# Short-sequence scores of two query tiles in one row-half visit, in an order that plans TensorE's operands as late

## The chip, the cores and the metric

One core of one Trainium2 chip runs the whole program in one launch. The metric is the device time of one execution in microseconds, as the median of several runs.

## What is computed

One layer of a hybrid encoder for two sequences, 256 and 512 rows of width 1024 in fp32, worked on together as 768 columns. Cut to what matters:

```
xn   = rmsnorm(x);  proj = xn @ w_in
y_a  = RWKV-7 mixer, 16 heads, one scan forward and one backward
y_b  = differential attention, 8 heads, partial rotary
h    = x + (sigmoid(ga) * (y_a @ proj_a) + sigmoid(gb) * (y_b @ proj_b)) @ w_out
y    = rmsnorm(h + relu(rmsnorm(h) @ w_mlp_in)**2 @ w_mlp_out)

def attend(qblk):                       # for each head, for each 128 queries
    s = einsum('bhcqd,bhckd->bhcqk', qblk, k)      # c = 0, 1; d = 64
    p = softmax(s, axis=-1)
    att = p[:, :, 0] - lam * p[:, :, 1]
    return einsum('bhqk,bhkv->bhqv', att, v)
```

## The kernel before, in words

The program is written once as a list of operations, each with the engines that could run it. A planner, `Plan.schedule`, then walks that list in Python with modelled durations and decides, for every engine, the order in which its operations are issued. On the chip every engine runs its list in that order and waits by semaphores. So no time of the model is on the chip; what the model leaves there is the order alone, and an operation that stands early in its engine's list holds up all that stand behind it until its operands are there.

What the planner goes by, as far as this case needs it:

- When an operation ends, each of its users becomes ready at that end plus `AFTER` of the user's engine (line 131); for TensorE that is 0.053 us.
- Among the operations that are ready, an engine takes the one with the smallest key: the stage's base number plus `SHIFT` of its label (line 577). On TensorE `SWITCH` (1.24, line 135) is added if the operation uses another tile shape of the array than the last one (128x128, the row halves 64x128, 128x64, 32x32).
- `BIAS` weighs the engines that could run an operation, and `LATE` (line 575) says how many pieces of the late work (the last 16 projections, then the product with proj_a) are put ahead of each attention head.

The stages in order of time:

1. The input is normalised and transposed (0 to 30 us), and the first projections run.
2. The RWKV stage, up to about 1085 us of the profile. Eight pairs of heads, four jobs each (two directions, two halves), 32 jobs in all. A job makes its operands (`front`), multiplies them on TensorE (`g1`), solves triangular systems (`solve`), and then runs through its six chunks (`duo`, `chain`). The solve goes from the products through a DMA to GpSimd, where it is 62 small tensor operations of 96 partitions (line 622, tiles named f), and by a DMA back into tiles that VectorE transposes (line 677). Its result is first read by TensorE in products of 128x64 array tiles, then 32x32. A chunk of `chain` is a pair of 128x64 products whose result is copied and read by the next pair. `fill` (line 658) zeroes the first state of a sequence on GpSimd. Projections of 128x384 columns (tile x) fill TensorE in between; `proj_shift` also adds shifted columns on GpSimd (128x256), and `front` adds one 128x384 tile there for every second job.
3. The attention stage (to about 1290 us), with the late work between. For each head and each 128 queries: scores of both halves c, their maxima on VectorE, exponentials on ScalarE, the difference, transposes, and the product with v. The two score products contract over 64 rows each and lie in different row halves of the array, where they run side by side; each fills a PSUM bank of its own. This is done twice per head for the short sequence (256 columns) and four times for the long one (512).
4. proj_b, w_out and the second norm (to about 1480 us), then the MLP.

A transpose on TensorE is line 698, every other matmul line 693. An fp32 product shows as two matmul rows, one of the projections (fp32r) as one.

Of the kernel before, what the change touches and what calls it, by code (L numbers as in the profile page):

```python
# [19 lines left out]
P = 128  # L20
D = 1024
TP, TS = 256, 512
# [4 lines left out]
C = 64  # L27
# [100 lines left out]
    return out  # L128


AFTER = dict(pe=0.053, act=0.034, dve=0.033, pool=0.077, sp=0.026)
TAIL = dict(dve=0.09, act=0.1, pool=0.03)
HELD = 0.012
PORT = 0.16
SWITCH = 1.24


DEBUG = {}
# [168 lines left out]
class Plan:  # L307
# [99 lines left out]
    def schedule(self):  # L407
# [14 lines left out]
        def blocked(o):  # L422
            for b in o.take:
                p = b.pool
                if p.lock or (p.ordered and p.next != b.n):
                    return p
                if b.pin is None and len(p.free) < sum(c.pool is p for c in o.take) or b.pin is not None and all(i != b.pin for _, i in p.free):
                    return p
            return None

# [35 lines left out]
        def choose(e, t):  # L466

            switch = lambda o: SWITCH * (e == "pe" and o.forms[e][2][0] != clock.tile)
            for k, n, r, o in sorted((o.key + TURN * turns(o, e) + switch(o), o.n, r, o) for r, o in avail[e] if r <= t + 1e-3):
# [12 lines left out]
        while len(order) < len(self.ops):  # L482
# [8 lines left out]
            if best is None:  # L491
                t, e = ways[0]
                best = min((x for x in avail[e] if x[0] <= t + 1e-3), key=lambda x: (x[1].key, x[1].n))
            r, o = best
            withdraw(o)
            p = blocked(o)
# [3 lines left out]
            for b in o.take:  # L500
                p = b.pool
# [39 lines left out]
            for s in o.next:  # L541
                s.wait -= 1
                for f in s.forms:
                    s.ready[f] = max(s.ready[f], clk[e] if e == f == "pe" else end + AFTER[f])
                if not s.wait:
# [3 lines left out]
            for b in o.blocks:  # L549
# [4 lines left out]
                if not b.left:  # L554
                    p = b.pool
# [16 lines left out]
WSTEP = 2  # L572
LATEKEY = 1.0
NLATE = 16
LATE = (4, 4, 4, 3, 3, 4, 4, 2)
REGIONS = dict(h=352, x=18816, f=12304, g1=6400, g2=15336)
SHIFT = {'proja': 3.64, 'rotate': -7.5, 'vs': -19.94, 'attn': -2.04, 'solve': -1.61, 'attend': -3.24, 'kkn': -4.92, 'proj': 4.76, 'g1': 1.9, 'g2': -1.95, 'chain': 1.9, 'norm': -6.88, 'x': -4.47, 'const': -7.99, 'lora': -10.39, 'front': 0.93, 'duo': -2.19, 'finish': -0.48, 'extra': 0.92, 'head': 3.89, 'projb': -6.52, 'wout': 18.65, 'mlp': -1.8}
BIAS = {'x': {'dve': -0.25, 'act': 0.68, 'pool': -0.82}, 'a': {'dve': 2.31, 'pool': 5.49, 'act': -0.17}, 'b': {'dve': 0.49, 'pool': 4.32, 'act': -0.19}, 'c': {'act': -0.05, 'pool': 1.31, 'dve': 0.09}}
RINGS = dict(fq=1, wraw=3, w=3, tst=3, X=2, g2r=2, vs=2, ik=3, sa=2, mk=1, y3=1, fo=2, v=2, k=2, r=2, lora=1, lr=1, py=1, cr=1)


def layer(tc, I, O, mark=None):
# [6 lines left out]
    size = lambda a: int(np.prod(a.shape[1:]))  # L589
# [93 lines left out]
    def mm(out, lhsT, rhs, start=True, stop=True, after=()):  # L683

        n, m, k = size(rhs), size(lhsT), lhsT.shape[0]
        if rhs.dtype == F32R:
            us, tail = max(0.118, n / 2400 + 0.0135), 0.25
        else:
            us, tail = 2 * max(n / 1200 + 0.005, 0.112 if m > 64 else 0.058), 0.165
        tile = tuple(next(x for x in (32, 64, 128) if y <= x) for y in (k, m))  # L690
        row, col = lhsT.quarter()[1], out.quarter()[1]
        slot = {(C, P): row // 2, (P, C): col // 2, (C, C): row // 2 * 2 + col // 2, (32, 32): row}.get(tile, 0)
        emit = lambda: TE.matmul(chip(out), lhsT=chip(lhsT), rhs=chip(rhs), start=start, stop=stop)  # L693
        pl.op([("pe", us, emit, (tile, rhs.dtype != F32R, slot))], [lhsT, rhs], [out], tail=tail, after=after)
        return pl.ops[-1]
# [12 lines left out]
    new = pl.block  # L708
# [6 lines left out]
    def bank(shape, co=()):  # L715
        return new(PS, shape, co=co)

    halves = [slice(h * HALF, (h + 1) * HALF) for h in range(2)]
    H0, H1 = slice(0, C), slice(C, P)
# [12 lines left out]
    o = 0  # L732
    for n, src, a, b in (
# [8 lines left out]
        so, w = PAR[src]  # L742
# [209 lines left out]
    extra = [QK0 + 4 * g for g in range(4)]  # L952
# [333 lines left out]
    pe_ = [pool_b([P, TS], 3) for i in range(2)]  # L1286
    pmx = pool_b([P, 4], 4)
# [3 lines left out]
    def load_head(h):  # L1291
# [17 lines left out]
            cpy(v[:, u : u + 3], ps)  # L1309
        return res + [v]  # L1310

    def attend(h, q, k, v):
        at("attend", h, key=200.0 + h)
        oT = yb[h]
        for t0, n in ((0, TP), (TP, TS)):
            nk = n // P
            for qt in range(nk):
                qo = slice(qt % 2 * P, qt % 2 * P + P)
                if qt % 2 == 0:
                    ah = new(pah, [P, 4, TP])  # L1320
                qs = slice(t0 + qt * P, t0 + (qt + 1) * P)
                ks = slice(t0, t0 + n)
                ms = new(pmx, [P, 4])
                mx, sm = ms[:, 0:2], ms[:, 2:4]
                e = [new(pe_[c], [P, TS])[:, 0:n] for c in range(2)]
                sc = [bank([P, n], [e[1], ms])]
                sc.insert(0, bank([P, n], [e[0], ms, sc[0]]))
                for c in range(2):
                    R = slice(c * C, (c + 1) * C)
                    mm(sc[c], q[R, qs], k[R, ks])  # L1330
                for c in range(2):
                    reduce(mx[:, c : c + 1], sc[c], ALU.max)
                ts(mx, mx, -0.125, None, ALU.mult, ALU.bypass)
                for c in range(2):
                    act(e[c], sc[c], AF.Exp, scale=0.125, bias=mx[:, c : c + 1], accum_out=sm[:, c : c + 1])
                recip(sm)
                tt(sm[:, 1:2], sm[:, 1:2], nlam, ALU.mult)
                scale(e[1], sm[:, 1:2])
                stt(e[0], e[0], sm[:, 0:1], e[1], ALU.mult, ALU.add)
                ps = bank([P, nk, P], [ah])  # L1340
                for u in range(nk):
                    tr(ps[:, u], e[0][:, u * P : (u + 1) * P])
                cpy(ah[:, 0:nk, qo], ps)
                if qt % 2 == 0:
                    continue
                ps = bank([P, TP], [oT])
                for u in range(nk):
                    kt = t0 // P + u
                    mm(ps, v[:, kt], ah[:, u], u == 0, u == nk - 1)
                q0 = t0 + (qt - 1) * P  # L1350
                cpy(oT[:, q0 : q0 + TP], ps)
        sq = new(psq, [P, T])
        tt(sq, oT, oT, ALU.mult, *AB)
        for b in range(2):
            ps = bank([P, HALF])
            mm(ps, ones, sq[:, halves[b]])
            act(sq[:, halves[b]], ps, AF.Ln, scale=1.0 / P, bias=eps[:, 2:3])
        act(sq, sq, AF.Exp, scale=-0.5)
        tt(oT, oT, sq, ALU.mult, *AB)
# [61 lines left out]
    for now in range(8):  # L1421
        for _ in zip(range(LATE[now]), more):
            pass
# [23 lines left out]
    for h in range(8):  # L1447
# [4 lines left out]
        for b in range(2):  # L1452
            c = halves[b]
# [41 lines left out]
    pss = [bank([P, 512]) for t in range(6)]  # L1495
    tok = [slice(t * P, (t + 1) * P) for t in range(6)]
    for k in range(KD):
        w = load_rows(I["wo"][0, :, k, :])
# [4 lines left out]
    pss = [bank([P, 512]) for t in range(6)]  # L1503
# [19 lines left out]
    for fb in range(NFB):  # L1523
        at("mlp", fb, key=600.0 + fb)
        hid = new(pmg, [P, 4, 2, T])
        for f in range(4):
            ps = gemm(load_w(I["w1"][4 * fb + f]), hn, [hid])
            for b in range(2):
                c = halves[b]
# [4 lines left out]
        for half in range(2):  # L1534
            c = slice(half * 512, (half + 1) * 512)
# [68 lines left out]
```

## Time and profile before

| | before |
|---|---|
| median of 3 runs | 1998.9 us |
| lowest and highest | 1997.29 and 1999.33 us |
| the profiled execution's own time | 1998.35 us |
| its span, first to last instruction | 1996.5 us |
| TensorE busy | 1938.1 us (97%) |
| VectorE, ScalarE, GpSimd busy | 1259.4, 871.9, 828.5 us |
| mean granted clock of TensorE | 0.989 |

Busy time on TensorE is taken from modelled ends that reach past the next start, so 97% is not an array at its peak. Lines are those of the kernel above. PE is TensorE's matmuls, PEld its weight loads, DVE is VectorE, ACT ScalarE, POOL GpSimd, SP the queue of most DMAs.

### The profile page before, as it was taken

How to read it: one execution, taken by the hardware profiler on the slowest of the kernel's cores; microseconds unless marked ns; L12 is line 12 of the kernel's file. 1: busy time of each engine (PE TensorE's matmuls, PEld its weight loads, DVE VectorE, ACT ScalarE, POOL GpSimd, SP SyncE). 2: the span in 40 equal slices, each digit the busy share in tenths (PEclk: the TensorE clock that was granted, in tenths of full speed). 3: DMA queues.
4: the chain of work that ended last, by engine and by line, in shares of the span. 5: the costliest groups of instructions: out<-in, count | busy, mean ns of one | idle time of the engine just before them, and what ended most of it. 6: DMA issues, size and time to landing. Idle time of an engine off the chain costs nothing.

```text
span 1996.5 us, 36368 instructions
## 1 busy us (share of the span) xinstructions
PE 1938.1 (97%) x12698; PEld 1729.2 (87%) x12698; DVE 1259.4 (63%) x2750; ACT 871.9 (44%) x2178; POOL 828.5 (41%) x2177
## 2 busy tenths in 40 slices
PE   6999989999999999999999999999999999999998
PEld 6988879888888989889888776899899899989997
DVE  6977575666767677577534878574475555555545
ACT  5635465555656556565444778442221111111113
POOL 3278778786877878888770011011100000000000
PEclk9999999999999999999999999999999999999999
DMA  4133332222323232232343342254121111111111
GB/s 152 55 110 97 86 84 75 76 70 73 92 66 98 76 79 80 81 88 59 93 121 107 107 143 76 81 174 139 45 85 64 63 64 64 64 64 64 64 48 64
DMA packets 209787, 169.09 MB, mean 85 GB/s; under 512 B 106817, under 2 KB 176194, under 8 KB 209602
## 3 DMA queue, kind: packets, MB, share of 16 engines
q1 hardware_dynamic: 209602, 166.76, 28.1%
q8 instruction: 100, 1.64, 0.4%
q14 instruction: 85, 0.70, 0.1%
HBM read 137.97 MB, written 28.70 MB: 83 GB/s over the span
## 4 chain that ended last, share of the span: by engine, by line
PE 80%; DVE 11%; DMA 3%; ACT 2%; SPq 2%; issue 2%; POOL 0%; DVEq 0%; ACTq 0%; POOLq 0%
PE bank L693 78%; DVE g L622 3%; PE bank L698 2%; DVE x L622 2%; SPq L618 2%; DVE f L627 1%; DVE f L632 1%; DMA g<-dram 1%; DVE f L622 1%; DMA g<-in_w_in_dram 1%; DVE g L632 0%; DVE f L1012 0%; ACT f L669 0%; ACT x L638 0%; DVE g L677 0%
## 5 line engine op out<-in xcount | busy, mean ns | idle before, releaser
L693 PE MATMUL bank<-x 128*128 128x384 f32 (+1 forms) x5296 | 1146.9, 362 | 13.0 <-DVE x L622 4.6
L693 PEld LDWEIGHTS bank<-x 128*128 128x128 f32 x5296 | 929.6, 189 | 113.3 <-issue 18.9
L622 POOL TENSOR_TENSOR f<-f 96x60 f32<-96x60 f32 (+25 forms) x2081 | 758.9, 367 | 241.1 <-ACT f L638 41.5
L622 DVE TENSOR_TENSOR x<-g,x 128x256 fp32r<-128x256 f32 (+3 forms) x490 | 252.6, 522 | 159.7 <-ACT x L638 149.8
L693 PE MATMUL bank<-f,g 128*128 128x384 f32 x1920 | 338.2, 337 | 1.6 <-ACT f L669 1.6
L693 PEld LDWEIGHTS bank<-f,g 128*128 128x128 f32 x1920 | 336.1, 187 | 2.6 <-ACT f L669 1.9
L638 ACT ACTIVATE x<-g 128x256 fp32r<-128x256 f32 (+2 forms) x336 | 149.8, 453 | 351.6 <-PE bank L693 282.0
L622 DVE TENSOR_TENSOR g<-bank,g 128x128 f32<-128x128 f32 (+4 forms) x380 | 178.0, 479 | 179.2 <-PE bank L693 143.2
L638 ACT ACTIVATE g<-bank 64x128 f32<-64x128 f32 (+6 forms) x659 | 203.8, 324 | 189.3 <-PE bank L693 152.8
L622 POOL TENSOR_TENSOR g<-g 128x512 f32<-128x512 f32 (+1 forms) x9 | 15.4, 1711 | 592.3 <-DVE g L622 580.8
L693 PE MATMUL bank<-g,f 128*128 128x64 f32 (+3 forms) x1568 | 245.1, 293 | 4.5 <-DVE g L622 2.1
L693 PEld LDWEIGHTS bank<-g,f 128*128 128x128 f32 x1568 | 218.1, 191 | 27.0 <-DVE f L622 3.8
L622 DVE TENSOR_TENSOR g<-g 128x384 f32<-128x384 f32 (+6 forms) x234 | 116.7, 502 | 86.2 <-ACT g L669 73.8
L669 ACT ACTIVATE g<-bank 128x384 f32<-128x384 f32 x96 | 46.3, 491 | 246.5 <-PE bank L693 246.1
L638 ACT ACTIVATE f<-bank 128x192 f32<-128x192 f32 (+6 forms) x268 | 95.4, 387 | 109.9 <-PE bank L693 95.8
L693 PEld LDWEIGHTS bank<-g,g 64*128 64x128 f32 (+1 forms) x1728 | 119.7, 193 | 22.5 <-ACT g L638 10.7
L693 PE MATMUL bank<-g,g 64*128 64x128 f32 (+1 forms) x1728 | 136.5, 287 | 1.4 <-ACT g L638 1.4
L639 DVE CAST x<-g 128x384 fp32r<-128x384 f32 (+2 forms) x156 | 56.6, 364 | 54.7 <-PE bank L693 40.4
L698 PE MATMUL bank<-h,g 128*128 128x128 f32 x392 | 67.9, 294 | 19.0 <-DVE g L647 14.3
L693 PE MATMUL bank<-f 128*128 128x256 f32 (+2 forms) x352 | 86.0, 483 | 0.0
L693 PEld LDWEIGHTS bank<-g 32*32 32x32 f32 (+2 forms) x1378 | 54.8, 130 | 34.8 <-DVE g L677 14.4
L693 PE MATMUL bank<-g 32*32 32x32 f32 (+3 forms) x1378 | 73.9, 225 | 10.5 <-DVE g L677 9.0
(80 smaller groups left out, 1356.8 us busy)
## 6 DMA issues: line engine op xcount, KB each, us to landing
g<-in_w_in_dram SPq DMA_DIRECT2D x268, 128.0 KB
g<-in_w_dram SPq DMA_DIRECT2D x128, 256.0 KB
f<-dram SPq DMA_DIRECT2D x112, 192.0 KB
dram<-g SPq DMA_DIRECT2D x80, 192.0 KB
g<-in_x_dram SPq DMA_DIRECT2D x12, 512.0 KB
g<-dram SPq DMA_DIRECT2D x32, 192.0 KB
f<-dram SPq DMA_DIRECT2D x32, 144.0 KB
g<-in_pb_dram SPq DMA_DIRECT2D x16, 256.0 KB
```

Of the source, the lines that this page charges most:

```text
L618: pl.op([("sp", us, lambda: nc.sync.dma_start(out=chip(out), in_=chip(in_)), None)], [in_], [out], n / 250e3, tail)
L622: form = lambda x: (NAME[x], cost(x, (a, b), out), lambda: x.tensor_tensor(out=chip(out), in0=chip(a), in1=chip(b), op=op), None)
L627: emit = lambda: V.tensor_scalar(out=chip(out), in0=chip(a), scalar1=chip(s1), scalar2=chip(s2), op0=o0, op1=o1)
L632: emit = lambda: V.scalar_tensor_tensor(out=chip(out), in0=chip(a), scalar=chip(s), in1=chip(b), op0=o0, op1=o1)
L638: S: ("act", cost(S, (a,), out), lambda: S.activation(out=chip(out), in_=chip(a), func=AF.Copy, scale=1.0), None),
L639: V: ("dve", cost(V, (a,), out), lambda: V.tensor_copy(out=chip(out), in_=chip(a)), None),
L669: S.activation(out=chip(out), in_=chip(a), func=fn, scale=chip(scale), **k)
L693: emit = lambda: TE.matmul(chip(out), lhsT=chip(lhsT), rhs=chip(rhs), start=start, stop=stop)
L698: pl.op([("pe", 0.112, lambda: TE.transpose(chip(out), chip(a), chip(ident)), ((P, P), True, 0))], [a, ident], [out], tail=0.165)
```

## The change

The scores move into a function of their own. For the short sequence it is called once for two query tiles: each of the two banks then holds both tiles' scores of one half c, and the four products are issued in turn between the row halves, in one visit to that array shape. For the long sequence it works on one tile as before. `blocked` lets an operation take several buffers of one ordered pool at once, since the visit takes two tiles' buffers. In the planner TensorE's operands count as ready 0.4 us later than before, and a change of array shape costs a key 2.44 instead of 1.24. `LATE` has 5 instead of 3 at the fifth head. The `SHIFT` and `BIAS` tables have new values.

```diff
-AFTER = dict(pe=0.053, act=0.034, dve=0.033, pool=0.077, sp=0.026)
+AFTER = dict(pe=0.453, act=0.034, dve=0.033, pool=0.077, sp=0.026)
...
-SWITCH = 1.24
+SWITCH = 2.44
...
-                if p.lock or (p.ordered and p.next != b.n):
+                n = sum(c.pool is p for c in o.take)
+                if p.lock or (p.ordered and not p.next <= b.n < p.next + n):
                     return p
...
-LATE = (4, 4, 4, 3, 3, 4, 4, 2)
+LATE = (4, 4, 4, 3, 5, 4, 4, 2)
...
+    def scores(qs, k, co):
+
+        n = size(k)
+        w = TS // n
+        pss = []
+        for _ in range(0, len(qs), w):
+            for c in range(2):
+                pss.append(bank([P, min(w, len(qs)), n], co + pss))
+        pss.reverse()
+        last, out = (), []
+        for i, q in enumerate(qs):
+            out.append([pss[i // w * 2 + c][:, i % w] for c in range(2)])
+            for c, R in ((0, H0), (1, H1)):
+                last = [mm(out[-1][c], q[R], k[R], after=last)]
+        return out
...
+            GQ = 2 if n == TP else 1
...
-                ms = new(pmx, [P, 4])
+                if qt % GQ == 0:
+                    mss = [new(pmx, [P, 4]) for _ in range(GQ)]
+                    es = [[new(pe_[c], [P, TS])[:, 0:n] for c in range(2)] for _ in range(GQ)]
+                    scs = scores([q[:, t0 + (qt + i) * P : t0 + (qt + i + 1) * P] for i in range(GQ)], k[:, t0 : t0 + n], [x for e in es for x in e] + mss)
+                ms, e, sc = mss[qt % GQ], es[qt % GQ], scs[qt % GQ]
                 mx, sm = ms[:, 0:2], ms[:, 2:4]
-                e = [new(pe_[c], [P, TS])[:, 0:n] for c in range(2)]
-                sc = [bank([P, n], [e[1], ms])]
-                sc.insert(0, bank([P, n], [e[0], ms, sc[0]]))
-                for c in range(2):
-                    R = slice(c * C, (c + 1) * C)
-                    mm(sc[c], q[R, qs], k[R, ks])
```

The order is where most of the change lies. The first place is TensorE in the eighteenth job, three steps of its `chain`: a step is the 128x64 pair, and the 128x384 rows between are projections. Before:

```order
L693 MATMUL bank_75<-g_91,f_97 128x64 x2
L693 MATMUL bank_80<-x_88 128x384
L693 MATMUL bank_77<-x_88 128x384 x3
L693 MATMUL bank_80<-x_88 128x384
L693 MATMUL bank_75<-g_91,f_97 128x64 x2
L693 MATMUL bank_80<-x_88 128x384 x2
L693 MATMUL bank_77<-x_88 128x384
L693 MATMUL bank_75<-g_91,f_97 128x64 x2
```

With the change:

```order
L694 MATMUL bank_80<-g_91,f_97 128x64
L694 MATMUL bank_77<-x_88 128x384 x3
L694 MATMUL bank_82<-x_88 128x384 x3
L694 MATMUL bank_80<-g_91,f_97 128x64 x2
L694 MATMUL bank_77<-x_88 128x384 x3
L694 MATMUL bank_82<-x_88 128x384 x3
L694 MATMUL bank_80<-g_91,f_97 128x64 x2
```

Three to five projections between two steps have become six.

The second place is TensorE at the scores of the second head's short sequence (128x256 from one tile f; the rows of x4 are the product with v of other query tiles, 128x128 of line 698 and 699 the transposes). Before, two visits:

```order
L693 MATMUL bank_79<-f_97 128x256
L693 MATMUL bank_77<-f_97 128x256
L693 MATMUL bank_80<-x_88 128x384
L693 MATMUL bank_81<-f_97 128x256 x4
L693 MATMUL bank_78<-g_91,f_97 128x384
L698 MATMUL bank_80<-h_85,g_105 128x128 x4
L693 MATMUL bank_76<-x_88 128x384 x2
L693 MATMUL bank_81<-f_97 128x256
L693 MATMUL bank_82<-f_97 128x256
```

With the change, one visit at a like place:

```order
L694 MATMUL bank_79<-f_97 128x256 x4
L694 MATMUL bank_76<-f_97 128x256
L694 MATMUL bank_81<-f_97 128x256
L694 MATMUL bank_76<-f_97 128x256
L694 MATMUL bank_81<-f_97 128x256
L694 MATMUL bank_78<-x_88 128x384
L699 MATMUL bank_75<-h_85,g_105 128x128 x4
```

The two pairs of score products now follow each other, in the same two banks.

The third place is GpSimd in the thirteenth job's solve (the 96-partition rows), where the two zero fills and the 128x384 sum of another job's `front` stand between. Before:

```order
L622 TENSOR_TENSOR f_97<-f_97 96x52
L622 TENSOR_TENSOR f_97<-f_97 96x2x26
L658 MEMSET g_91 64x128
L622 TENSOR_TENSOR f_97<-f_97 96x50
L658 MEMSET g_91 64x128
L622 TENSOR_TENSOR f_97<-f_97 96x2x25
L622 TENSOR_TENSOR f_97<-f_97 128x384
```

With the change:

```order
L623 TENSOR_TENSOR f_97<-f_97 96x63
L659 MEMSET g_91 64x128
L623 TENSOR_TENSOR f_97<-f_97 96x3x21
L623 TENSOR_TENSOR f_97<-f_97 96x60
L659 MEMSET g_91 64x128
L623 TENSOR_TENSOR f_97<-f_97 96x3x20
L623 TENSOR_TENSOR f_97<-f_97 128x384
```

All three stand nine or ten solve operations further back in GpSimd's list.

## Rows read from the trace of the kernel before

**Rows 1.** The page: span, busy time of each engine, TensorE in 40 slices.
```profile
span 1996.5 us, 36368 instructions
PE 1938.1 (97%) x12698; PEld 1729.2 (87%) x12698; DVE 1259.4 (63%) x2750; ACT 871.9 (44%) x2178; POOL 828.5 (41%) x2177
PE   6999989999999999999999999999999999999998
```
**Rows 2.** Busy time by stage: stretch, length, each engine's us (instructions), PEclk, DMA share, GB/s.
```profile
95.00:1050.00 955.00, 924.90 (x7357) 834.53 (x7356) 630.04 (x1488) 524.49 (x1392) 751.40 (x2093) 0.98 0.31 84
1085.00:1290.00 205.00, 204.61 (x1060) 152.69 (x1060) 159.57 (x400) 147.55 (x357) 23.58 (x20) 1.00 0.32 98
1290.00:1480.00 190.00, 187.62 (x995) 173.74 (x995) 110.44 (x188) 61.27 (x124) 21.31 (x15) 1.00 0.36 115
1480.00:1997.00 517.00, 508.18 (x2565) 462.63 (x2563) 271.48 (x490) 67.21 (x137) 2.70 (x2) 0.99 0.19 62
```
**Rows 3.** POOL's waits, 95 to 1050 us: waiter, releaser: total us, times, longest.
```profile
POOL f L622 <- DVE f L622: 21.7, 14, 2.8
POOL g L658 <- PE bank L693: 14.6, 7, 4.9
...
POOL f L622 <- PE bank L693: 0.2, 1, 0.2
```
**Rows 4.** POOL in order of time around a wait: start, us, instructions, idle before.
```profile
490.08 6.36 POOL L622 TENSOR_TENSOR f<-f 96x31 f32<-96x31 f32 x15
498.57 1.58 POOL L622 TENSOR_TENSOR f<-f 128x384 f32<-128x384 f32 x2 [2.13 <-DVE f L622]
```
**Rows 5.** Waits of PE's matmuls, 110 to 1085 us.
```profile
PE bank L693 <- DVE g L677: 9.0, 7, 2.9
...
PE bank L693 <- DVE g L632: 0.2, 1, 0.2
```
**Rows 6.** Waits of PE's weight loads, 110 to 1085 us.
```profile
PEld bank L693 <- ACT g L638: 20.3, 68, 1.2
...
PEld bank L693 <- DVE g L632: 0.4, 1, 0.4
```
**Rows 7.** PE in order of time at the fifteenth job.
```profile
571.93 0.54 PE L693 MATMUL bank<-g 128*64 128x32 f32 x12 [2.55 <-DVE g L677]
...
578.46 0.63 PE L693 MATMUL bank<-g,f 128*128 128x64 f32 x4
578.89 0.77 PE L693 MATMUL bank<-x 128*128 128x384 f32 x3
579.50 0.60 PE L693 MATMUL bank<-g,f 128*128 128x64 f32 x4
```
**Rows 8.** PE in order of time in the attention stage.
```profile
1101.25 1.89 PE L693 MATMUL bank<-f 128*128 128x256 f32 x8
1102.97 0.81 PE L693 MATMUL bank<-g,f 128*128 128x384 f32 x2
...
1103.98 0.60 PE L693 MATMUL bank<-x 128*128 128x384 f32 x2
1104.50 0.70 PE L693 MATMUL bank<-f 64*128 64x256 f32 x4
1105.14 3.09 PE L693 MATMUL bank<-x 128*128 128x384 f32 x16
1108.13 0.63 PE L698 MATMUL bank<-h,g 128*128 128x128 f32 x4
...
1124.76 4.79 PE L693 MATMUL bank<-x 128*128 128x384 f32 x26
1129.38 0.60 PE L698 MATMUL bank<-h,g 128*128 128x128 f32 x4
```
**Rows 9.** Two stretches with a lower granted clock; columns as in rows 2.
```profile
380.00:390.00 10.00, 7.86 (x61) 6.44 (x62) 7.97 (x17) 5.15 (x15) 8.34 (x20) 0.66 0.34 100
440.00:460.00 20.00, 17.11 (x133) 15.21 (x131) 3.57 (x9) 5.91 (x19) 15.70 (x55) 0.83 0.42 121
```

More of the change, by code (lines that the diff above doesn't have):

```diff
@@ L424, in blocked @@
                 p = b.pool
-                if p.lock or (p.ordered and p.next != b.n):
+                n = sum(c.pool is p for c in o.take)
+                if p.lock or (p.ordered and not p.next <= b.n < p.next + n):
                     return p
-                if b.pin is None and len(p.free) < sum(c.pool is p for c in o.take) or b.pin is not None and all(i != b.pin for _, i in p.free):
+                if b.pin is None and len(p.free) < n or b.pin is not None and all(i != b.pin for _, i in p.free):
                     return p
@@ L574 @@
 NLATE = 16
-LATE = (4, 4, 4, 3, 3, 4, 4, 2)
+LATE = (4, 4, 4, 3, 5, 4, 4, 2)
 REGIONS = dict(h=352, x=18816, f=12304, g1=6400, g2=15336)
-SHIFT = {'proja': 3.64, 'rotate': -7.5, 'vs': -19.94, 'attn': -2.04, 'solve': -1.61, 'attend': -3.24, 'kkn': -4.92, 'proj': 4.76, 'g1': 1.9, 'g2': -1.95, 'chain': 1.9, 'norm': -6.88, 'x': -4.47, 'const': -7.99, 'lora': -10.39, 'front': 0.93, 'duo': -2.19, 'finish': -0.48, 'extra': 0.92, 'head': 3.89, 'projb': -6.52, 'wout': 18.65, 'mlp': -1.8}
-BIAS = {'x': {'dve': -0.25, 'act': 0.68, 'pool': -0.82}, 'a': {'dve': 2.31, 'pool': 5.49, 'act': -0.17}, 'b': {'dve': 0.49, 'pool': 4.32, 'act': -0.19}, 'c': {'act': -0.05, 'pool': 1.31, 'dve': 0.09}}
+SHIFT = {'proja': 3.68, 'rotate': -5.61, 'vs': -20.91, 'attn': -7.05, 'solve': -2.9, 'attend': -2.08, 'kkn': -4.32, 'proj': 4.7, 'g1': 1.71, 'g2': -1.95, 'chain': 1.9, 'norm': -6.7, 'x': -4.47, 'const': -8.17, 'lora': -9.73, 'front': 0.93, 'duo': -2.05, 'finish': -2.34, 'extra': 0.37, 'head': 2.79, 'projb': -6.57, 'wout': 17.42, 'mlp': -0.98}
+BIAS = {'x': {'dve': -0.67, 'act': 0.68, 'pool': -1}, 'a': {'dve': 2.31, 'pool': 5.25, 'act': 0.35}, 'b': {'dve': 0.49, 'pool': 4.03, 'act': -0.19}, 'c': {'act': 0.57, 'pool': 1.4, 'dve': 0.09}}
 RINGS = dict(fq=1, wraw=3, w=3, tst=3, X=2, g2r=2, vs=2, ik=3, sa=2, mk=1, y3=1, fo=2, v=2, k=2, r=2, lora=1, lr=1, py=1, cr=1)
@@ L1320, in attend @@
                     ah = new(pah, [P, 4, TP])
-                qs = slice(t0 + qt * P, t0 + (qt + 1) * P)
-                ks = slice(t0, t0 + n)
-                ms = new(pmx, [P, 4])
-                mx, sm = ms[:, 0:2], ms[:, 2:4]
-                e = [new(pe_[c], [P, TS])[:, 0:n] for c in range(2)]
-                sc = [bank([P, n], [e[1], ms])]
-                sc.insert(0, bank([P, n], [e[0], ms, sc[0]]))
-                for c in range(2):
-                    R = slice(c * C, (c + 1) * C)
-                    mm(sc[c], q[R, qs], k[R, ks])
+                if qt % GQ == 0:
[3 more added lines that the diff above has]
+                ms, e, sc = mss[qt % GQ], es[qt % GQ], scs[qt % GQ]
+                mx, sm = ms[:, 0:2], ms[:, 2:4]
                 for c in range(2):
```

## The prediction

> **What bounds the kernel now.** The page comes first [rows 1]: TensorE (PE) is busy for 97% of the span, so only work taken off PE, or time in which it waits, can shorten the run. The stretches tell where such time lies [rows 2]. From 1480 us on the matmuls follow each other without a break (the first and last slices of the whole run aside), and between 1085 and 1480 PE misses 2.8 us in 395. Between 95 and 1050 us it misses 30 of 955. That RWKV stage is the one to look at, and GpSimd (POOL) has to be looked at with it: its 2093 instructions keep it busy for 751 us. Its waits there are ten rows, 56.5 us in 45 times [rows 3]. So 955 - 751 - 56.5 = 147 us, or 0.07 us behind each instruction, is what it leaves between two operations even when nothing holds it. POOL is thus full to 94% (898 of 955 us), nearly as full as PE. In the stage two engines run in step: PE waits for a solve that POOL ended late [rows 7], and POOL's solve stands still because an interleaved operation at the head of its list waits for somebody else, as the 128x384 sum that comes 2.13 us late [rows 4].
>
> PE's own waits between 110 and 1085 us: its matmuls show thirteen rows, 25.4 us in 35 times [rows 5]; its weight loads, without the two rows called issue, fifteen rows, 73.4 us in 182 times [rows 6]. The first is too little, since a matmul's row reaches past the start of the next and hides short waits; the second is too much, since a load can wait while the array still works. I take the middle, about 49 us.
>
> **The change part by part.** *Visits to other array shapes.* Counted in the order, PE changes the shape 378 times before and 352 times now: 13 visits fewer, 9 to the row halves (8 of them the merged scores) and 4 to 32x32. One visit's price is read at two tiles of 256 columns [rows 8]. The visit takes 1105.14 - 1104.50 = 0.64 us for two rounds of 256 columns, and a round is 0.215 (eight in 1.72 from 1101.25 to 1102.97), so 0.21 is extra inside. A 128x384 row takes 0.178 (26 in 4.62); the two ahead of the visit take 0.52 instead of 0.36, the sixteen behind it 2.99 instead of 2.85. So a visit costs 0.21 us at least and 0.51 at most; those neighbours also change data type and may wait, so I take 0.4, nearer the upper end because all three effects stand at every visit that I can read. 13 x 0.4 = 5.2 us off (2.7 to 6.6). The score products themselves stay as many.
>
> The rule that speaks against counting these 5.2 is the Trainium skill's, "TensorEngine Tiling (Array Packing)", section "PSUM Bottleneck": tiling speeds up TensorE but not the emptying of PSUM, which may then become the bound. In the attention stage the rows say otherwise, PE 204.6 of 205 us against 160 for VectorE [rows 2]. By the rule the eight merged visits would give nothing and the term would be 2.0 instead of 5.2.
>
> *Changes of data type.* PE's fp32 rows between fp32r rows at the full shape grow by 22 visits (by the order). A step of four 128x64 passes and the three projections behind it: the latter take 579.50 - 578.89 = 0.61 instead of 0.53 [rows 7], so 0.08 each: 1.8 us more (0 to 3.5).
>
> *Start.* Eight more matmuls stand ahead of the first products that feed POOL: 8 x 0.178 = 1.4 us more.
>
> *The 0.4 us.* Where PE's order had three projections between two steps of a chain (65 of 95 places) it now has six (76 of 98), so 0.53 us of other work became 1.07. What a later place of 0.4 us can absorb: a wait shorter than that goes, a longer one loses 0.4. The 35 waits that matmuls show are the long ones; a row's end stands some 0.16 us past the next start (578.89 + 0.77 against 579.50 [rows 7]) and hides that much of each, so 25.4 - 35 x 0.24 = 17 us of them would stay and at most 49 - 17 = 32 us can go. Nothing excludes that new ones come. I take a little under two thirds, 20 us, because the rest is lateness of whole microseconds that comes from POOL, as the seven waits for the transposes of a solve, 9.0 us, up to 2.9 at once [rows 5].
>
> *The granted clock.* 0.98 over 955 us [rows 2] is some 19 us of PE's time lost (14 to 24 by rounding). The lower level (1.2 GHz) shows where PE had just waited: 0.66 in the ten us in which it was busy for 7.86, 0.83 in the twenty that hold a three-us wait [rows 9]. With fewer waits I take a quarter back: 5 us (0 to 15).
>
> *POOL, which must keep up.* It gets no work off, and 18 operations more, all behind 1050 us where it is idle. In its list 26 of 29 zero fills and 51 of 63 shifted sums stand later among the solve's operations, by 8 and 6 of these in the middle, while PE's products that feed the sums stand where they stood; of the fourteen 128x384 sums, the ones in VectorE's debt, 10 stand later and 3 earlier. At 955 / 2093 = 0.46 us an instruction that is 2.8 to 3.7 us more for the data to arrive, against waits of 1.3 us on average and 4.9 at most [rows 3]. So much of its 56.5 us should go, and it needs to lose only some 24 for PE's gain.
>
> *SP, VectorE, ScalarE.* SP issues 1373 DMAs in both, in another sequence; no wait of PE names a DMA, and I count nothing. VectorE gets 30 operations more and ScalarE 48 fewer, at 66% and 55% busy in the stage [rows 2]: nothing. If that cover is gone, VectorE's 30 at 1259.4 / 2750 = 0.46 us [rows 1] are 14 us spread over the run.
>
> **Sum.** The profiled execution took 1998.35 us, 0.03% under the median shown. 1998.35 - 5.2 + 1.8 + 1.4 - 20 - 5 = 1971.4, said as **1971 us**. All at the good ends: 1998.35 - 6.6 + 1.4 - 32 - 15 = 1946.
>
> **Rivals.** *Only the short waits go.* Most of the 49 us lie in the long ones, 25.4 + 35 x 0.16 = 31, and they may be POOL's lateness. Then two thirds of the other 18 go and no clock comes back: 1998.35 - 5.2 + 3.2 - 12 = 1984. For it speaks that seven waits for a solve hold 9.0 us [rows 5]; against it, that POOL's own list is looser now.
>
> *POOL sets the pace.* If POOL's waits are the work of VectorE's and ScalarE's queues rather than of PE's place, they stay: 14 of the 45 are for VectorE's tile f, 21.7 us [rows 3]. Then the stage keeps its 955 us, PE's waits only move to the solves, and what is left is behind 1085 us: 11 changes of shape fewer in the attention stage, 5.5 x 0.4 = 2.2. That gives 1996, no change.
>
> *POOL gets slower, and with it the run.* The first products of the solves now stand 1 to 6 us of PE's work earlier in 30 of 32 jobs (counted in the order, 2.7 in the middle), so PE has less to do while POOL finishes. POOL's 1984 solve operations have no fixed price: the same 128x384 sum and its neighbour took 1.58 us for two [rows 4], the small ones 6.36 / 15 = 0.42 in one stretch, and the whole stage 751 / 2093 = 0.36. If more of VectorE's operations fall together with them and the mean rises by 3% (0.011 us), POOL needs 22 us more, nothing hides it because PE waits at the next solve, and the time is 1998.35 + 22 - 2.2 = 2018. It decides from the point at which POOL's longer operations eat up what its shorter waits give, a rise of 7.5% (56.5 / 751) at most. The Trainium skill's "SBUF — State Buffer", section "SBUF: two separate sides", gives a reason: VectorE and GpSimd share a port pair under an exclusive lock, and who starts second is blocked for the whole instruction. No row here shows a lock, only the spread; by that rule the 30 operations that VectorE gains could be the ones that hit.
>
> **Numbers.** About 0.2% (4 us) is what a measurement can tell from no change. Chances: forecast 0.57, only the short waits 0.17, POOL sets the pace 0.13, POOL slower 0.13. So faster 0.74, same 0.13, slower 0.13. The range reaches from 1950, just above all the good ends together, to 1997, which takes in the third case; it leaves out the slower case and the little below, under 0.2.
>
> **What would show it.** Right: in the stage that now ends near 1085 us PE's waits fall below 30 us (weight loads below 45), POOL's below 35, the last solve ends on POOL near 1025 instead of 1050, and the stretches at the lower clock get fewer; in the attention stage a head shows one row of eight passes 64x256 in about 1.07 us. Wrong: PE's waits for the transposes grow beyond 9 us while those for copies shrink (POOL sets the pace), or POOL's busy time before the last solve rises above 751 us (POOL slower). The MLP must not move; if it does, the cause is none of these.

## The result, and the profile after

The change takes 1961.61 us (median of 5 runs, 1960.89 to 1962.67) where the kernel before took 1998.9 beside it: ratio 0.9815 [0.9801, 0.983], 37 us faster. The forecast was 1971, 27 us faster. From the planner's `blocked` on, line numbers are one higher than in the rows of before (L622 is now L623, L693 is L694).

The page: span, busy times, TensorE in 40 slices (answers to [rows 1]).

```profile
span 1959.8 us, 36374 instructions
PE 1911.8 (98%) x12698; PEld 1732.9 (88%) x12698; DVE 1271.8 (65%) x2780; ACT 849.1 (43%) x2130; POOL 850.8 (43%) x2195
PE   6989999999999999999999999999999999999998
```

PE's instructions are as many, and it is busy for 26 us less: a busy matmul includes its time at the lower clock and short stalls hidden under its modelled end. The stretches of the stages, shifted with the end of the RWKV stage (answers to [rows 2]; columns as there):

```profile
95.00:1023.00 928.00, 909.47 (x7405) 841.24 (x7404) 641.07 (x1513) 517.16 (x1375) 760.87 (x2100) 0.99 0.33 89
1055.00:1260.00 205.00, 202.13 (x1060) 154.50 (x1059) 161.22 (x400) 151.83 (x365) 30.48 (x27) 1.00 0.31 95
1260.00:1450.00 190.00, 188.39 (x1007) 176.39 (x1007) 115.75 (x202) 48.52 (x100) 27.84 (x20) 1.00 0.38 118
1450.00:1955.00 505.00, 502.20 (x2531) 456.64 (x2529) 268.64 (x486) 61.71 (x128) 2.70 (x2) 1.00 0.19 61
```

The first row is the one that changed: 7405 matmuls in 928 us, where before 7357 took 955. The others pass as many matmuls per us as before, or a few more. POOL's waits between 100 us and its last solve at 1022.9 (answers to [rows 3]; before, the same stretch up to its last solve at 1049.6 held 55.8 us in 44 times):

```profile
POOL f L623 <- DVE f L623: 7.8, 8, 1.6
POOL f L623 <- ACT f L639: 5.4, 5, 1.3
POOL f L623 <- DVE f L633: 4.6, 7, 1.2
POOL g L659 <- PE bank L694: 1.2, 2, 0.9
POOL x L623 <- ACT x L639: 1.0, 2, 0.8
POOL x L623 <- DVE x L640: 0.5, 2, 0.2
```

20.5 us in 26 times. From 95 us on, as in [rows 3], it is 28.5 in 27, because one more wait of 7.9 ends at 95.08. The zero fills' wait for PE (14.6 in seven) is 1.2 in two; the wait for VectorE's sums (21.0 in thirteen from 100 us on) is 7.8 in eight. A row of POOL in order of time where [rows 4] had a 2.13 us hole:

```profile
483.71 22.26 POOL L623 TENSOR_TENSOR f<-f 96x66 f32<-96x66 f32 x47
505.91 0.20 POOL L659 MEMSET g<- 64x128 f32 x1
506.07 4.08 POOL L623 TENSOR_TENSOR f<-f 96x8 f32<-96x8 f32 x10
```

No operation here waits. PE's matmuls between 110 and 1055 us wait 13.5 us in 30 times, after 25.4 in 35 [rows 5]. Five of their ten rows:

```profile
PE bank L694 <- ACT x L639: 3.0, 6, 0.7
PE bank L694 <- ACT g L639: 2.7, 4, 1.6
PE bank L694 <- DVE x L623: 1.7, 6, 0.4
...
PE bank L694 <- DVE g L678: 1.0, 2, 0.7
...
PE bank L694 <- DMA g<-dram: 0.2, 1, 0.2
```

The fourth is the wait for a solve's transposes, 9.0 us in seven times before. The weight loads, without the two rows called issue, wait 42.2 us in 111 times, after 73.4 in 182 [rows 6]. Three of them:

```profile
PEld bank L694 <- DVE x L623: 8.0, 24, 0.8
...
PEld bank L694 <- ACT g L639: 6.3, 15, 1.8
...
PEld bank L694 <- DVE g L678: 2.7, 8, 1.0
```

The second of these, the copies of the chain, was 20.3 us in 68 times. The rows called issue, left out on both sides, went the other way, from 17.7 us to 25.8. At the fifteenth job, where the first product of a solve waited 2.55 us [rows 7], the same products (128x32) follow projections with a wait of 0.29 us, and more projections stand between them and the 32x32 ones:

```profile
544.64 3.39 PE L694 MATMUL bank<-x 128*128 128x384 f32 x18
548.32 0.54 PE L694 MATMUL bank<-g 128*64 128x32 f32 x12 [0.29 <-DVE g L678]
548.79 0.97 PE L694 MATMUL bank<-x 128*128 128x384 f32 x4
549.69 0.39 PE L694 MATMUL bank<-g 32*32 32x32 f32 x24
```

The merged scores, in the attention stage (answers to [rows 8]):

```profile
1141.37 1.14 PE L694 MATMUL bank<-f 64*128 64x256 f32 x8
1142.44 3.05 PE L694 MATMUL bank<-x 128*128 128x384 f32 x16
```

Eight passes in 1.07 us where two visits of four took 2 x 0.64 = 1.28: the 0.21 inside a visit is paid once. And the two stretches that were at a lower clock [rows 9] hold the full 2.4 GHz:

```profile
380.00:390.00 10.00, 9.07 (x80) 7.70 (x77) 8.85 (x21) 6.16 (x18) 8.38 (x20) 1.00 0.37 117
440.00:460.00 20.00, 19.94 (x161) 18.39 (x160) 12.96 (x31) 9.69 (x29) 16.55 (x51) 1.00 0.35 97
```

By the clock's records of these two executions the lower level held, up to the last matmul, for 37.5 us before and for 23.9 now; now all but 3.4 of it lies before 117 us.

**Where the time went.** On PE, I compared each matmul's distance to the next with the lower quartile of its kind (shape, type, place in a visit) in the trace of before: from 30 us on, stalls fell from 116.3 to 90.6 us (-26), the excess at the lower clock from 15.3 to 7.0 (-8), and the rest, visits and types, by 2. That split is an estimate: it hangs on the base and on how small an excess still counts as a stall. With other choices the stalls fall by 10 to 26 us and the rest by 19 to 3; only the clock's 8 stays. On POOL, from 100 us to the last solve: 949.6 us were 747.2 busy + 55.8 waits + 146.6 between operations; now 922.9 are 756.5 + 20.5 + 145.9. So POOL lost 35.3 us of waits, got 9.3 us busier, and ended its last solve 26.7 us earlier; PE's last product of a solve came 32 us earlier (1069.1 to 1037.0). From the first product with w_out (the first 128x512 row, at 1386.46 and now 1351.74 us) to the end of the last matmul it took 601.7 and now 600.5 us: the MLP did not move.

### The profile page after: what moved, and what is told of

It is laid out like the page before. It is cut to its first block, busy times and chain, and to the rows that moved or that the text cites. A ratio compares the mean times of both kernels' runs of the same rounds, so it can differ in the third digit from the quotient of the medians.

```text
span 1959.8 us, 36374 instructions
## 1 busy us (share of the span) xinstructions
PE 1911.8 (98%) x12698; PEld 1732.9 (88%) x12698; DVE 1271.8 (65%) x2780; ACT 849.1 (43%) x2130; POOL 850.8 (43%) x2195
## 4 chain that ended last, share of the span: by engine, by line
PE 61%; DVE 5%; POOL 2%; ACT 1%; issue 1%; DMA 1%; SPq 0%; POOLq 0%; ACTq 0%; DVEq 0%
PE bank L694 59%; POOL f L623 2%; PE bank L699 2%; DVE g L623 1%; DVE x L623 1%; DVE f L633 0%; ACT g L670 0%; DVE g L633 0%; DVE f L628 0%; DVE f L623 0%; DVE f L1013 0%; SPq L619 0%; DVE g L1271 0%; ACT g L649 0%; DMA g<-dram 0%
## 5 line engine op out<-in xcount | busy, mean ns | idle before, releaser
L694 PE MATMUL bank<-x 128*128 128x384 f32 (+1 forms) x5296 | 1153.2, 363 | 11.8 <-DVE x L623 5.2
L694 PEld LDWEIGHTS bank<-x 128*128 128x128 f32 x5296 | 931.5, 189 | 112.1 <-issue 20.6
L623 POOL TENSOR_TENSOR f<-f 96x60 f32<-96x60 f32 (+26 forms) x2081 | 764.9, 370 | 220.1 <-ACT f L639 37.8
L623 DVE TENSOR_TENSOR x<-g,x 128x256 fp32r<-128x256 f32 (+3 forms) x482 | 252.0, 528 | 137.8 <-ACT x L639 125.4
L694 PE MATMUL bank<-f,g 128*128 128x384 f32 x1920 | 338.0, 337 | 1.6 <-ACT f L670 1.6
L694 PEld LDWEIGHTS bank<-f,g 128*128 128x128 f32 x1920 | 336.0, 187 | 2.5 <-ACT f L670 1.9
L623 DVE TENSOR_TENSOR g<-bank,g 128x128 f32<-128x128 f32 (+4 forms) x380 | 177.2, 479 | 185.0 <-PE bank L694 143.4
L639 ACT ACTIVATE x<-g 128x256 fp32r<-128x256 f32 (+2 forms) x320 | 142.0, 449 | 335.0 <-PE bank L694 298.0
L639 ACT ACTIVATE g<-bank 128x128 f32<-128x128 f32 (+6 forms) x647 | 198.5, 323 | 191.7 <-PE bank L694 150.9
L623 POOL TENSOR_TENSOR g<-g 128x512 f32<-128x512 f32 (+1 forms) x12 | 18.8, 1571 | 585.4 <-DVE g L623 575.2
L694 PE MATMUL bank<-g,f 128*128 128x64 f32 (+2 forms) x1568 | 235.8, 286 | 3.4 <-ACT g L639 2.2
L694 PEld LDWEIGHTS bank<-g,f 128*128 128x128 f32 x1568 | 226.1, 191 | 10.6 <-ACT g L639 2.8
L623 DVE TENSOR_TENSOR g<-g 128x384 f32<-128x384 f32 (+6 forms) x231 | 112.6, 490 | 78.5 <-ACT g L670 68.6
L694 PEld LDWEIGHTS bank<-g,g 64*128 64x128 f32 (+1 forms) x1728 | 116.3, 188 | 20.6 <-issue 11.7
L694 PE MATMUL bank<-g,g 64*128 64x128 f32 (+1 forms) x1728 | 131.4, 282 | 1.9 <-DVE g L640 1.3
L640 DVE CAST x<-g 128x256 fp32r<-128x256 f32 (+2 forms) x172 | 62.1, 361 | 56.9 <-PE bank L694 43.7
L694 PE MATMUL bank<-f 128*128 128x256 f32 (+2 forms) x352 | 84.6, 478 | 1.9 <-DVE f L640 1.0
L699 PE MATMUL bank<-h,g 128*128 128x128 f32 x392 | 68.0, 293 | 17.7 <-DVE g L648 11.7
L670 ACT ACTIVATE g<-g 128x512 f32<-128x512 f32 (+4 forms) x90 | 49.3, 550 | 71.5 <-DVE g L623 60.7
L699 PEld LDWEIGHTS bank<-h,g 128*128 128x128 f32 x392 | 50.2, 149 | 30.7 <-DVE g L648 12.1
```

Source lines behind the costliest of these rows:

```text
L623: form = lambda x: (NAME[x], cost(x, (a, b), out), lambda: x.tensor_tensor(out=chip(out), in0=chip(a), in1=chip(b), op=op), None)
L639: S: ("act", cost(S, (a,), out), lambda: S.activation(out=chip(out), in_=chip(a), func=AF.Copy, scale=1.0), None),
L640: V: ("dve", cost(V, (a,), out), lambda: V.tensor_copy(out=chip(out), in_=chip(a)), None),
L670: S.activation(out=chip(out), in_=chip(a), func=fn, scale=chip(scale), **k)
L699: pl.op([("pe", 0.112, lambda: TE.transpose(chip(out), chip(a), chip(ident)), ((P, P), True, 0))], [a, ident], [out], tail=0.165)
```

## The experiments

The theory on trial: operands counted as late let PE and POOL run past each other's lateness (LATE). Its rivals: POOL's pace decides, and PE's place matters only through POOL's list (POOL PACES); the merged scores do it; the tables do it, or the luck of one order. Times are medians, ratios against before on the same chip; before took 1996.56 us beside the runs a, 1995.96 beside b and 1996.04 beside c and d.

### One part alone, or one part undone

**a1_late_alone**, before with one number changed:

```diff
-AFTER = dict(pe=0.053, act=0.034, dve=0.033, pool=0.077, sp=0.026)
+AFTER = dict(pe=0.453, act=0.034, dve=0.033, pool=0.077, sp=0.026)
```

> The kernel before with nothing but TensorE's operands planned 0.4 us later (AFTER pe 0.453). Theory LATE (the later place of TensorE's users takes the waits away, on TensorE and, since the zero fills and sums move back in GpSimd's list, on GpSimd too): 1965 to 1980 us, TensorE's waits for solves under 3 us, the last solve on GpSimd at 1030 or earlier, GpSimd's waits before it under 40 us. Rival TABLES (the new SHIFT, BIAS and LATE values were fitted to the chip and carry the gain): 1992 to 2005, waits as before. Rival VISITS (fewer changes of array shape): 376 changes here against 378, so 1998.

Measured: 1978.58 us, 0.99 [0.9886, 0.9915]. The number alone gives 18 of the 37 us. The last solve ended at 1030.0 us and POOL's waits before it were 31.8 us, both as expected; PE's waits for the transposes of the solves were 5.6 us, not under 3.

**a2_late_undone**, the change with the same number put back to 0.053.

> The changed kernel with TensorE's operands planned as before (AFTER pe 0.053); scores, SWITCH and tables stay new. LATE: 1988 to 2002, chain steps again three projections apart, waits for the transposes of the solve back near 9 us. TABLES: 1962 to 1970. VISITS: 378 changes of shape again, so 1972 (26 changes at 0.2 us and the clock they cost).

Measured: 2002.75 us, 1.0025 [1.0012, 1.0039], just above the range of LATE. Without the number nothing is left of the gain. PE's waits for the transposes were 4.0 us, not near 9: they do not go with the time.

**a3_tables_alone**, before with the new tables:

```diff
-LATE = (4, 4, 4, 3, 3, 4, 4, 2)
+LATE = (4, 4, 4, 3, 5, 4, 4, 2)
...
+SHIFT = {'proja': 3.68, 'rotate': -5.61, 'vs': -20.91, 'attn': -7.05, 'solve': -2.9, 'attend': -2.08, 'kkn': -4.32, 'proj': 4.7, 'g1': 1.71, 'g2': -1.95, 'chain': 1.9, 'norm': -6.7, 'x': -4.47, 'const': -8.17, 'lora': -9.73, 'front': 0.93, 'duo': -2.05, 'finish': -2.34, 'extra': 0.37, 'head': 2.79, 'projb': -6.57, 'wout': 17.42, 'mlp': -0.98}
```

> The kernel before with the new SHIFT, BIAS and LATE values alone. LATE: 1994 to 2006, since the order still leaves three projections between two chain steps, and 404 changes of shape against 378 cost 5 us more. TABLES: 1965 to 1980.

Measured: 2013.6 us, 1.0068 [1.005, 1.0087]: 17 us slower, outside both ranges. POOL's waits between 95 and 1050 us in this run, its three longest rows:

```profile
POOL f L622 <- DVE f L622: 24.5, 14, 5.6
POOL x L622 <- ACT x L638: 13.2, 3, 7.4
POOL g L658 <- PE bank L693: 10.7, 6, 3.8
```

The new values are no gain by themselves.

**a4_scores_alone**, before with `scores`, the calls in `attend` and `blocked`, and the old numbers; the order of the RWKV stage is that of before.

```diff
+            GQ = 2 if n == TP else 1
...
+                    scs = scores([q[:, t0 + (qt + i) * P : t0 + (qt + i + 1) * P] for i in range(GQ)], k[:, t0 : t0 + n], [x for e in es for x in e] + mss)
```

> The kernel before with the scores of two query tiles in one visit alone (function scores, blocked); all constants old. The order up to the attention stage is the same, 364 changes of shape against 378, so seven visits fewer at 0.4 us: 1995.5 to 1997 by LATE and by VISITS alike, with the whole difference behind 1085 us; 1998.5 if the emptying of the banks sets the pace of that stage.

Measured: 1997.5 us, 1.0007 [0.9994, 1.002]. 14 changes of shape fewer, 7 visits x 0.4 = 2.8 us, did not show.

**b1_scores_undone**, the change with the old scores in `attend` (and the old `blocked`) and its other numbers kept.

```diff
-                    scs = scores([q[:, t0 + (qt + i) * P : t0 + (qt + i + 1) * P] for i in range(GQ)], k[:, t0 : t0 + n], [x for e in es for x in e] + mss)
+                for c in range(2):
+                    R = slice(c * C, (c + 1) * C)
+                    mm(sc[c], q[R, qs], k[R, ks])
```

> The changed kernel with the scores as before (one query tile a visit); all constants new. The order of the RWKV stage is the changed one to the instruction, changes of array shape 372 against 352. Theory VISITS (0.4 us for each visit): ten visits more, 1965.6, all of it behind 1070 us. Rival NOTHING (as the scores alone did on the kernel before: 1997.5 against 1996.6): 1961 to 1963, the longer visits are paid back as waits for softmax pieces in the same stage.

Measured: 1964.39 us (1961.64 to 1966.13, 5 runs), 0.9837 [0.9819, 0.9856]. 2.8 us behind the change, with ranges that touch (1961.64 against 1962.67), and between the two expectations. The merged scores are a small part of the 37 us, if any.

**b2_tables_undone**, the change with the old LATE, SHIFT and BIAS.

> The changed kernel with the old SHIFT, BIAS and LATE values; AFTER, SWITCH and the scores stay new. Operands late alone gave 1978.6. Theory FIT (the tables are worth something only with the late operands, which is why alone they cost 17 us): 1972 to 1980, that is 10 to 18 us over the change. Rival SWITCH (the rest of the gain is SWITCH and the scores, 352 changes of shape here too): 1960 to 1966.

Measured: 1972.32 us, 0.9877 [0.986, 0.9895]. With late operands the tables are worth 11 us, which is no more than one order differs from the next (c1 below). Against a1 (1978.58), which lacks `SWITCH` and the merged scores too, it is 6 us.

### How late is late

**b3_late_850** and **b4_late_253**, the change with another number:

```diff
-AFTER = dict(pe=0.453, act=0.034, dve=0.033, pool=0.077, sp=0.026)
+AFTER = dict(pe=0.853, act=0.034, dve=0.033, pool=0.077, sp=0.026)
```

> The changed kernel with TensorE's operands planned 0.8 us late instead of 0.4 (AFTER pe 0.853): eight projections between two chain steps. LATE with saturation: TensorE's waits fall a little more, but 92 microseconds-long chains get longer and the planner's order drifts from what the tables were fitted to: 1960 to 1975. If each 0.1 us later went on paying as the first 0.4 did (41 us in all from 2002.8): 1930 to 1945.

Measured: 1969.31 us, 0.9865 [0.9847, 0.9883]: saturation.

> The changed kernel with TensorE's operands planned 0.2 us late (AFTER pe 0.253): five projections between two chain steps. LATE, in proportion: half way between 2002.8 (undone) and 1961.6, 1975 to 1990; waits for the solve's transposes between 2 and 9 us. FIT of the tables to exactly this value: nearer to undone, 1990 to 2003.

Measured: 1998.08 us, 1.0006 [0.9995, 1.0017]: nothing of the half that LATE expected, but the range of the rival. PE's waits for the transposes were 1.6 us, fewer than in a1, which is 20 us faster.

**c1_late_443**, the change with pe=0.443, to see what the luck of one order is worth.

> The changed kernel with 0.443 in place of 0.453: no theory expects anything of the hundredth itself. It makes the planner choose another order and shows how much of a difference is the luck of one order: 1958 to 1966 if little, up to 1985 if the tables were fitted to one order alone.

Measured: 1972.42 us, 0.9883 [0.9856, 0.991]. One hundredth of a us in the planner, and 10.8 us are lost. The time follows no slope: 0.253 gives none of it, 0.443 and 0.853 some 25 us with the change's other parts, and 0.453 with the same parts some 35. Between two steps of a chain stand 5 projections in the middle at 0.253, 6 at 0.443 and 0.453, 8 at 0.853. Why five give nothing in the time is read from POOL's trace below.

### Does POOL set the pace

**d1_pool_margin** plans POOL's operands late, on before:

```diff
+LAG = 2.0
...
-                    s.ready[f] = max(s.ready[f], clk[e] if e == f == "pe" else end + AFTER[f])
+                    s.ready[f] = max(s.ready[f], clk[e] if e == f == "pe" else end + AFTER[f] + LAG * (f == "pool" and e in ("pe", "act", "dve")))
```

> The kernel before, TensorE's operands planned as before (0.053), but what GpSimd takes from TensorE, ScalarE or VectorE planned 2 us later. So far GpSimd's busy time in the RWKV stage was the same in all runs (755 to 772 us) while its waits went from 76 down to 19 us, and the time with them. Theory POOL PACES (the gain of the change is that GpSimd no longer stands behind interleaved operations whose operands are missing): its waits fall from 53 to under 30, 1970 to 1982 us, although chain steps stay three projections apart. Rival PE PACES (TensorE's own short waits are what the later operands took away): TensorE's waits stay near 49, 1993 to 2003.

Measured: 2000.87 us, 1.0029 [1.0017, 1.004], a miss for POOL PACES as I had put it. The three longest rows of POOL's waits between 95 and 1050 us:

```profile
POOL f L623 <- DVE f L633: 23.8, 17, 3.9
POOL f L623 <- DVE f L623: 16.4, 7, 4.1
POOL g L659 <- PE bank L694: 8.4, 5, 2.8
```

The waits for the zero fills shrank, from 14.6 to 8.4, and those for VectorE's scalar-tensor-tensor operations (L633, 5.4 before) took their place. A margin in POOL's list alone moves its waits to another producer. Since they did not shrink (58.3 us after 55.8), this run cannot tell whether shorter ones would have paid.

**d2_both_margins**, the change with the same two lines.

> The changed kernel with the same 2 us for what GpSimd takes from the other engines. POOL PACES: the 18 us that are left of its waits fall under 8, 1945 to 1957. PE PACES: 1958 to 1968, GpSimd's list only stands further back.

Measured: 1970.81 us, 0.9883 [0.9859, 0.9907]: 9 us slower than the change and in neither range; POOL's waits rose to 34.6 us instead of falling under 8.

**d3_pool_loaded**, the change with one product of the solve issued twice into the same tile at four of its steps, 128 operations more on POOL, the same result:

```diff
-            tt(tmp, tm[:, rr, jj : jj + 1].to_broadcast([NP_, n, w]), sa[:, jj, ss].unsqueeze(1).to_broadcast([NP_, n, w]), ALU.mult, SOLVE)
+            for _ in range(2 if i < 4 else 1):
+                tt(tmp, tm[:, rr, jj : jj + 1].to_broadcast([NP_, n, w]), sa[:, jj, ss].unsqueeze(1).to_broadcast([NP_, n, w]), ALU.mult, SOLVE)
```

> The changed kernel with the product of the first four of a solve's 31 steps made twice on GpSimd: 128 operations of up to 96x248 more, about 0.41 us each with the gap, 53 us. It computes the same. POOL PACES: 35 to 55 us of it show, 1997 to 2017. PE PACES: GpSimd's gaps swallow most, 1961 to 1975.

Measured: 2000.22 us, 1.002 [1.0005, 1.0034], 38.6 us over the change. The costliest group of POOL on the page (line, engine, operation, count, busy us, mean ns, idle before it), of the change:

```profile
L623 POOL TENSOR_TENSOR f<-f 96x60 f32<-96x60 f32 (+26 forms) x2081 | 764.9, 370 | 220.1 <-ACT f L639 37.8
```

and of this run:

```profile
L623 POOL TENSOR_TENSOR f<-f 96x60 f32<-96x60 f32 (+22 forms) x2209 | 795.0, 362 | 241.8 <-ACT f L639 38.2
```

128 operations more, 30.1 us more busy, and at 0.07 us behind each 9 us between them: 39 us given to POOL, 38.6 us more in the time. That the two agree so well is luck: POOL's stretch from 100 us to its last solve grew by 51.0 us (busy 27.6, waits 13.0, gaps 10.4), and 12.4 came back behind it. But PE did not swallow POOL's work as its rival had it; by the distances between its matmuls it spent 30 us more in stalls and 9 more at the lower clock. So in the change POOL sets the pace of the stage. No run loads POOL in the kernel before; for that one there are the rows of its trace, below.

### What the runs share

POOL's stretch from 100 us to its last solve, taken apart for every run (busy time and waits from the two views, the rest is what they leave), in the order of their times; PE's waits are those of its matmuls from 110 us to 30 us behind that solve:

| run | time | stretch | busy | waits | rest | PE's waits |
|---|---|---|---|---|---|---|
| the change | 1961.6 | 922.9 | 756.5 | 20.5 | 145.9 | 13.5 |
| b1_scores_undone | 1964.4 | 921.5 | 751.6 | 24.2 | 145.7 | 14.8 |
| b3_late_850 | 1969.3 | 931.0 | 758.6 | 26.9 | 145.5 | 21.3 |
| d2_both_margins | 1970.8 | 930.9 | 750.2 | 34.6 | 146.2 | 25.5 |
| b2_tables_undone | 1972.3 | 932.2 | 755.4 | 30.8 | 146.0 | 21.4 |
| c1_late_443 | 1972.4 | 930.0 | 753.4 | 30.4 | 146.1 | 20.7 |
| a1_late_alone | 1978.6 | 930.0 | 751.9 | 31.8 | 146.3 | 25.0 |
| a4_scores_alone | 1997.5 | 948.3 | 747.7 | 53.9 | 146.7 | 25.8 |
| b4_late_253 | 1998.1 | 957.0 | 743.0 | 66.3 | 147.7 | 33.4 |
| before | 1998.9 | 949.6 | 747.2 | 55.8 | 146.6 | 25.4 |
| d3_pool_loaded | 2000.2 | 973.9 | 784.1 | 33.5 | 156.3 | 34.7 |
| d1_pool_margin | 2000.9 | 948.9 | 744.2 | 58.3 | 146.4 | 28.0 |
| a2_late_undone | 2002.8 | 955.5 | 743.3 | 65.6 | 146.6 | 25.6 |
| a3_tables_alone | 2013.6 | 969.8 | 743.7 | 79.6 | 146.5 | 34.0 |

Leave out d3: busy time moves within 16 us, the rest within 3, the waits over 59, and the time with them. That alone proves no cause: the three columns add up to the stretch, so a longer stretch with the same work shows as waits, whatever made it longer. All runs with operands later by 0.39 us or more have POOL's waits at 20 to 35 us, all others at 54 to 80. PE's own waits tell less: a1 has those of before and is 18 to 20 us faster.

Where on POOL the waits stand says more. Its 32 solves follow each other without overlapping. In the kernel before, from the first operation of the first (93.7 us) to the end of the last (1049.6), 949.9 of 955.9 us lie inside a solve and 6.0 between two. Of its 56.6 us of waits there the solves' own 1984 operations have 0.6; all others stand before operations of other work in the list. So before the change too the stage was a chain on POOL, and waits of interleaved operations stretched it. The same reading for other runs (inside: POOL's waits between the first and the last operation of a solve; between: from the end of one solve to the start of the next, all 31 added up):

| run | number for PE | inside | between |
|---|---|---|---|
| before | 0.053 | 54.2 | 6.0 |
| d1_pool_margin | 0.053 | 57.9 | 5.8 |
| a1_late_alone | 0.453 | 19.9 | 18.7 |
| a2_late_undone | 0.053 | 49.0 | 23.8 |
| b4_late_253 | 0.253 | 33.4 | 43.3 |
| c1_late_443 | 0.443 | 20.3 | 18.5 |
| the change | 0.453 | 19.3 | 4.5 |
| b3_late_850 | 0.853 | 6.4 | 26.4 |

The last five differ in the number alone, and their waits inside the solves fall as it grows, at every step; 0.253 gives about half of what 0.453 gives there. What takes it back is holes between solves, at whose end POOL waits for a solve's own operands to land. The two of b4 (23.0 and 17.4 us from one solve to the next) and that of b3 (18.5) end with

```profile
263.21 1.40 POOL L623 TENSOR_TENSOR f<-f 96x31 f32<-96x31 f32 x3 [8.16 <-DMA f<-dram]
951.74 15.53 POOL L623 TENSOR_TENSOR f<-f 96x31 f32<-96x31 f32 x35 [7.61 <-DMA f<-in_tinit_dram]
808.68 19.06 POOL L623 TENSOR_TENSOR f<-f 96x31 f32<-96x31 f32 x43 [10.83 <-DMA f<-dram]
```

c1, a1 and b2 have one such hole each (13.0, 15.9 and 14.8 us); the change has none above 2.1. In a3 the solves took no longer than before (946.6 us in all); holes of 13.7 and 11.9 made its stage longer. What makes these operands late in one order and not in its neighbour was not tested.

## Why the prediction was right, and where it was off

- **The bound and the mechanism held.** The RWKV stage gave 32 of the 37 us, both engines' waits fell there, and the marks named came true: the last solve ended at 1022.9 (forecast near 1025), PE's matmuls wait 13.5 us (below 30), its loads 42.2 (below 45), POOL 20.5 (below 35), the transposes 1.0 instead of growing beyond 9.0, the merged visit takes 1.07 us, and the MLP stayed. One sign of being wrong came true as well: POOL was busy for 760.9 us from 95 us to its last solve, above 751. It was harmless, but not all of the 18 operations more stood "behind 1050 us": five more sums of tile x (128x256) now stand before the last solve, 3.9 us.
- **PE's waits, -20.** -26 by distances in the whole run; by the same reckoning, counting only stalls that a releaser ended, 48.7 became 30.6 in the RWKV stage, -18. I kept the long waits as POOL's lateness; they went too, from 9.0 to 1.0 for the solves. But these waits for the solves are no measure of the gain (a1 5.6, a2 4.0, b4 1.6 us). The bound of 32 held.
- **The clock, -5.** -8 in the two profiled executions. There were 15.3 us to get back, not 19, and about half came, not a quarter; the two stretches that I had read both came back whole.
- **Visits, -5.2, types +1.8, start +1.4.** Together -2.0 forecast, about -2 by distances on PE (as far as that split can tell). But the eight merged scores, 3.2 of the 5.2, gave 0 (a4) to 3 us (b1), not separable from zero. The Trainium skill, "TensorEngine Tiling (Array Packing)", section "PSUM Bottleneck", says that the emptying of PSUM may become the bound where tiling speeds TensorE up, which could take such a gain; PE is busy for 202.1 of 205 us in that stage against VectorE's 161.2, so the trace gives no sign of that, and a4's zero has no shown cause.
- **POOL as a condition instead of a term.** I wrote that POOL "needs to lose only some 24 for PE's gain" and left its waits out of the sum. They lost 35.3, its busy time took back 9.3, and its last solve ended 26.7 us earlier: the condition was met, with little to spare. d3 and the solves that stand end to end show that the stage goes at POOL's pace, so this was the chain to add up. It would not have given the 37 us alone: 5.4 more came between POOL's last solve and PE's last product of a solve, and some 5 behind that.
- **The rivals.** *Only the short waits go* falls with the solves' 9.0 to 1.0. *POOL sets the pace* was right in its first half (d3) and wrong in its second: the waits do not stay. *POOL gets slower* went a little its way: the mean of its operations rose from 367 to 370 ns on the page, far below the 7.5% from which it decides. Whether the lock of the Trainium skill's "SBUF — State Buffer", section "SBUF: two separate sides", has a part in that no row can tell; the group means of all runs lie between 362 and 372 ns.
- **What no row could tell.** Four small edits of the change (c1, b2, b3, d2) land at 1969 to 1972 us, just where the forecast stood; the change itself is 8 to 11 us under them, and b1, which keeps its order in the RWKV stage, 3. That part is luck, one order out of many like it: c1, b2 and b3 have a hole between two solves that it lacks, d2 longer waits inside them (30.2 us against 19.3).
- **Open.** How a later place on PE makes VectorE and ScalarE deliver to POOL in time was argued from the order, not isolated: d1 shows that a later place in POOL's list alone does not do it. The price of a change of shape in the planner (`SWITCH`) was not tried by itself: a1 lacks it, a2 has it and gains nothing, and with late operands b2 and a1 put it and the merged scores together at 6 us.

## What to carry to other kernels

Take each engine's stretch apart into busy time, waits and the gaps between its operations before calling one the bound: a POOL that is 79% busy with 2090 small operations was full, and the wait rows of that engine, not those of the busiest one, told where the gain was. Then ask where in its list a wait stands: inside a chain, before interleaved work, or between two links of it. Where an order is planned with modelled times, it can pay to let operands count as later than modelled on the engine that others wait for (18 us here by that alone); and run a neighbouring setting too, since one order can be 11 us luckier than the next.

## What the hardware showed that was not expected

- The gap between two of POOL's operations is as good as constant: 145.5 to 147.7 us for 2085 to 2093 instructions in thirteen runs, 0.07 us each, whatever the order; 128 operations more brought 10.4 us more of it, 0.08 each.
- POOL is slightly busier where it waits less: 743 to 748 us in the runs with over 50 us of waits, 750 to 759 in those with under 35 (without d3). Of the 9.3 us between before and the change, the solves' operations, as many as before, take 4.2 (687.9 to 692.1), and five more sums 3.9.
- TensorE's lower clock now shows mainly near the start. A wait of 3.47 us in the run of the change, then the stretch that holds it and the one behind it (columns as in [rows 2]):

```profile
107.36 2.93 PE L694 MATMUL bank<-x 128*128 128x384 f32 x8 [3.47 <-DVE x L623]
100.00:110.00 10.00, 6.06 (x28) 5.47 (x27) 9.73 (x22) 4.52 (x12) 8.49 (x20) 0.83 0.34 85
110.00:120.00 10.00, 9.32 (x38) 8.72 (x38) 5.39 (x11) 1.66 (x4) 8.51 (x22) 0.66 0.21 67
```

  PE is busy for only 6.06 of ten us, and in the next ten the mean granted clock is 0.66 although it works again.
